# The engines' instruction orders taken from another simulation: one flag of the framework's scheduler in a one-layer bidirectional encoder

## The chip, the core and the metric

The kernel runs on one core of a Trainium2 chip. The core has a matrix engine (PE, with its weight loads shown apart as PEld), a vector engine (DVE), an activation engine (ACT), a general engine (POOL) and a queue engine (SP) that issues transfers. Each engine takes its instructions strictly in the order in which the program gives them, and waits at the head of that order when an input isn't there. The metric is the device time of one execution in microseconds (us), as the median of several runs.

## What is computed

One encoder layer on 256 tokens of width 2048, all in float32, with one residual stream `x`:

```
h = rms_norm(x); proj = h @ w_in            # columns for three mixers and three gates
y_a = spatial_gating(u, v)                  # gMLP, 128-token chunks
y_b = hyena_mixer(b_cols)                   # long two-sided filters, by Fourier transform
y_c = rwkv7_mixer(c_cols)                   # 16 heads, one scan per direction
merged = sum_i sigmoid(gate_i) * (y_i @ w_branch_i)
x = x + merged @ w_out
h = rms_norm(x)
x = x + (silu(h @ w_gate) * (h @ w_up)) @ w_down      # inner width 5632
out = rms_norm(x)
```

## The kernel before

**Weights.** Every dense product reads its weights in pieces of four 128x128 blocks (256 KB). `wsplit` (lines 216 to 229) makes a piece ready: SP loads it into `w` (L221), ACT rounds it to a high half `wh` (L222), and DVE, or POOL for a share of the pieces, subtracts to get the low half `wl` (L226). `w`, `wh` and `wl` have five buffers each. A block then costs PE two or three matmuls: `dense_wide` (L259, L260) does one of 512 columns and one of 256, `dense_sum` the same (L270, L271), `dense` three of 256 (L239 to L241).

**Stages.** The gMLP mixer comes first (L1270 to L1272, then eight `dense_sum` products). Then Hyena: `weave` steps the generators `conv` and `filter_block` in turn, and between their steps lets `fill` trace some dense work of the next projections and merges. Then RWKV: eight groups of two heads go through five generators, `wkv_prep`, `wkv_scores`, `wkv_inverse`, `wkv_chain` and `wkv_norm`; `threads` steps them in turn, and after each step traces about four blocks of dense work (`ROUND = 4.0`). From there on (`merge_last`, `outproj`, `ffn`) it is dense products alone, with their evictions on DVE, ACT and POOL.

**One place in RWKV** that the argument needs. `wkv_inverse` runs a recursion of 15 steps on DVE, two small two-operand instructions a step, and sends its result off with four transfers issued by ACT:

```
z = Yt[:, :w * n].rearrange("p (c t) -> p c t", t=n)
first = V.tensor_tensor(z, ..., mult)                         # L736
V.tensor_tensor(Y[:, :w, k + 1:], Y[:, :w, k + 1:], z, add)    # L739
...
D.dma_start(d2[:, b, :, r, 16 * b:16 * b + 16], Y[...])        # L746, four, on ACT's queue
```

`wkv_norm` of an earlier group subtracts a mean on DVE (L916, after the matmul of L915), squares on ACT (L919), and sums the squares on PE (L921). `threads` steps `wkv_norm` ahead of `wkv_inverse`, so the norm's instructions are traced among those of the recursion.

**Who sets the order.** The kernel is traced instruction by instruction; that gives the program order. When the `TileContext` closes, the framework's list scheduler lays down the final order of each engine: it walks through a simulated time, and an engine that is free in it takes, of its instructions whose inputs and buffers are there in that simulation, the one traced first. So an instruction stands behind a later-traced one where the simulation had the later one ready first. The numbers of the simulation are used for nothing else: the instructions, their engines, their buffers and their semaphores' meaning stay as written. Two pins act on the order: `issue_after` puts what it encloses behind a named instruction of the same engine (in `threads`, every RWKV matmul behind the last dense one traced), and `keep_in_program_order` puts one instruction behind all that its engine has been given so far (L736's first of each recursion, the transposition at L754).

## Time and profile before

| | |
|---|---|
| median of 3 runs | 2004.01 us (2001.47 to 2006.61) |
| the profiled execution's own time | 2002.49 us |
| its span, first to last instruction | 2000.6 us |
| PE busy / PEld busy | 1890.1 us (94%) / 1676.9 us (84%) |
| DVE / ACT / POOL busy | 1389.2 (69%) / 1068.7 (53%) / 545.8 us (27%) |
| moved from HBM | 313.96 MB, 159 GB/s over the span |
| mean granted PE clock | 0.983 |

Busy is the time in which an engine ran at least one instruction. [...] What lies outside the span is 1.9 us of the execution's own time.

### The profile page before, as it was taken

How to read it: one execution, taken by the hardware profiler on the slowest of the kernel's cores; microseconds unless marked ns; L12 is line 12 of the kernel's file. 1: busy time of each engine (PE TensorE's matmuls, PEld its weight loads, DVE VectorE, ACT ScalarE, POOL GpSimd, SP SyncE). 2: the span in 40 equal slices, each digit the busy share in tenths (PEclk: the TensorE clock that was granted, in tenths of full speed). 3: DMA queues.
4: the chain of work that ended last, by engine and by line, in shares of the span. 5: the costliest groups of instructions: out<-in, count | busy, mean ns of one | idle time of the engine just before them, and what ended most of it. 6: DMA issues, size and time to landing. Idle time of an engine off the chain costs nothing.

```text
span 2000.6 us, 37495 instructions
## 1 busy us (share of the span) xinstructions
PE 1890.1 (94%) x13476; PEld 1676.9 (84%) x13476; DVE 1389.2 (69%) x2556; ACT 1068.7 (53%) x2142; POOL 545.8 (27%) x573
## 2 busy tenths in 40 slices
PE   8999999999879888898999999999999999999997
PEld 6788888879878777787898888888888888888886
DVE  7978798786775767667556777766666666655555
ACT  7665566555444454444545555555555555545443
POOL 3322322235654455544421121111111111100001
PEclk9999999999999999999999999999999999999998
DMA  7444444445333333333345565555555555666664
GB/s 259 160 168 150 135 157 154 137 138 187 125 112 94 97 99 97 110 99 91 107 158 186 186 229 189 187 190 190 190 190 190 190 190 190 189 186 186 188 186 136
DMA packets 215827, 320.38 MB, mean 160 GB/s; under 512 B 62198, under 2 KB 65784, under 8 KB 215640
## 3 DMA queue, kind: packets, MB, share of 16 engines
q1 hardware_dynamic: 165744, 301.93, 45.5%
q10 hardware_dynamic: 47864, 9.87, 2.5%
q0 software_dynamic: 2032, 6.18, 1.0%
q8 instruction: 106, 1.74, 0.3%
q14 instruction: 81, 0.66, 0.1%
HBM read 313.96 MB, written 3.93 MB: 159 GB/s over the span
## 4 chain that ended last, share of the span: by engine, by line
PE 50%; DVE 0%; DVEq 0%; ACT 0%; issue 0%; ACTq 0%
PE ps_dn L259 23%; PE ps_dn L260 12%; PE ps_big L259 8%; PE ps_big L260 4%; PE ps_dn L239 0%; PE ps_dn L240 0%; PE ps_dn L241 0%; PE ps_dn L257 0%; PE ps_dn L256 0%; DVE x L1458 0%; PE ps_inv L865 0%; DVEq L1473 0%; PE ps_ch L859 0%; PE ps_big L893 0%; PE ps_big L1415 0%; PE ps_big L898 0%
## 5 line engine op out<-in xcount | busy, mean ns | idle before, releaser
L222 ACT CAST wh<-w 128x512 fp32r<-128x512 f32 x1148 | 704.4, 620 | 569.6 <-PE ps_dn L259 260.0
L226 DVE TENSOR_TENSOR wl<-w,wh 128x512 fp32r<-128x512 f32 x945 | 719.7, 770 | 375.0 <-ACT wh L222 370.7
L226 POOL TENSOR_TENSOR wl<-w,wh 128x512 fp32r<-128x512 f32 x203 | 270.3, 1338 | 370.2 <-ACT wh L222 329.5
L259 PE MATMUL ps_dn<-gw,wh 128*128 128x512 f32 x704 | 246.3, 391 | 0.0
L259 PE MATMUL ps_big<-gw,wh 128*128 128x512 f32 x704 | 246.0, 391 | 0.0
L270 PE MATMUL ps_dn<-hw,wh 128*128 128x512 f32 x640 | 231.9, 401 | 11.9 <-DVE x L400 7.0
L259 PE MATMUL ps_dn<-hid,wh 128*128 128x512 f32 x660 | 233.2, 396 | 0.0
L239 PE MATMUL ps_dn<-hw,wh 128*128 128x256 f32 x688 | 213.4, 310 | 0.0
L241 PE MATMUL ps_dn<-hw,wl 128*128 128x256 f32 x688 | 199.1, 289 | 3.4 <-DVE wl L226 2.6
L240 PE MATMUL ps_dn<-hw,wh 128*128 128x256 f32 x688 | 199.2, 289 | 0.0
L260 PE MATMUL ps_dn<-hid,wl 128*128 128x256 f32 x704 | 198.4, 282 | 0.0
L260 PE MATMUL ps_dn<-gw,wl 128*128 128x256 f32 x704 | 197.3, 280 | 0.0
L260 PE MATMUL ps_big<-gw,wl 128*128 128x256 f32 x704 | 197.1, 280 | 0.0
L271 PE MATMUL ps_dn<-hw,wl 128*128 128x256 f32 x640 | 179.8, 281 | 0.0
L259 PEld LDWEIGHTS ps_dn<-gw,wh 128*128 128x128 f32 x704 | 131.7, 187 | 28.9
L259 PEld LDWEIGHTS ps_big<-gw,wh 128*128 128x128 f32 x704 | 131.6, 187 | 28.9
L270 PEld LDWEIGHTS ps_dn<-hw,wh 128*128 128x128 f32 x640 | 121.1, 189 | 39.6 <-ACT th L1348 5.6
L259 PEld LDWEIGHTS ps_dn<-hid,wh 128*128 128x128 f32 x660 | 124.0, 188 | 30.0
L239 PEld LDWEIGHTS ps_dn<-hw,wh 128*128 128x128 f32 x688 | 134.5, 195 | 6.4 <-issue 2.9
L241 PEld LDWEIGHTS ps_dn<-hw,wl 128*128 128x128 f32 x688 | 134.0, 195 | 4.8 <-DVE wl L226 3.0
L240 PEld LDWEIGHTS ps_dn<-hw,wh 128*128 128x128 f32 x688 | 134.5, 195 | 1.8
L260 PEld LDWEIGHTS ps_dn<-gw,wl 128*128 128x128 f32 x704 | 133.1, 189 | 0.1
(404 smaller groups left out, 3706.9 us busy)
## 6 DMA issues: line engine op xcount, KB each, us to landing
w<-in_wgu_dram SPq DMA_DIRECT2D x352, 256.0 KB, 3.0
w<-in_wgt_dram SPq DMA_DIRECT2D x192, 256.0 KB, 3.0
w<-in_wdn_dram SPq DMA_DIRECT2D x176, 256.0 KB, 2.8
w<-in_wc_dram SPq DMA_DIRECT2D x108, 256.0 KB, 3.0
w<-in_wb_dram SPq DMA_DIRECT2D x96, 256.0 KB, 3.0
w<-in_wbr_dram SPq DMA_DIRECT2D x96, 256.0 KB, 2.7
w<-in_wo_dram SPq DMA_DIRECT2D x64, 256.0 KB, 3.1
w<-in_wav_dram SPq DMA_DIRECT2D x32, 256.0 KB, 3.6
```

The source lines that it names most:

```text
L222: nc.scalar.copy(wh[:, :m], w[:, :m])
L226: e.tensor_tensor(wl[:, :m], w[:, :m], wh[:, :m].bitcast(F32), ALU.subtract)
L239: mm(ps, wh[:, i, :], xh[:, k, :], start=(k == 0), stop=False)
L240: mm(ps, wh[:, i, :], xl[:, k, :], start=False, stop=False)
L241: self.last = mm(ps, wl[:, i, :], xh[:, k, :], start=False, stop=(k == nk - 1))
L259: mm(ps, wh[:, i, :], xk.rearrange("p a t -> p (a t)"), start=(k == 0), stop=False)
L260: mm(ps[:, :T], wl[:, i, :], xk[:, 0, :], start=False, stop=(k == nk - 1))
L270: mm(ps, wh[:, i, :], x[:, k].rearrange("p a t -> p (a t)"), start=(k == 0), stop=False)
L271: mm(ps[:, :T], wl[:, i, :], x[:, k, 0, :], start=False, stop=(k == nk - 1))
```

## The change

One argument of the context is set. The scheduler then walks the timeline simulation, which holds sequencers, engines, transfer queues and PE's clock as separate resources, instead of its plain model. The kernel's text, and so the program order, stays the same.

```
-    with tile.TileContext(nc) as tc:
+    with tile.TileContext(nc, schedule_with_timeline_sim=True) as tc:
         Build(tc, aps, out).run()
```

## Rows read from the trace of the kernel before

**Rows 1.** Stages: window; busy of PE, PEld, DVE, ACT, POOL; granted clock; DMA.

```profile
57.00:128.00 71.00, 64.09 (x355) 54.73 (x355) 61.64 (x137) 45.65 (x93) 25.00 (x27) 0.95 0.46 156
128.00:467.00 339.00, 320.46 (x1938) 282.86 (x1939) 275.49 (x475) 201.50 (x408) 103.01 (x71) 0.99 0.44 149
467.00:1010.00 543.00, 477.35 (x5306) 442.06 (x5305) 363.51 (x800) 254.55 (x575) 284.75 (x303) 0.96 0.36 109
1010.00:1023.00 13.00, 13.00 (x126) 12.58 (x126) 6.90 (x16) 5.37 (x11) 3.60 (x4) 1.00 0.39 131
1023.00:1987.00 964.00, 963.41 (x5555) 845.70 (x5553) 628.43 (x1033) 520.15 (x974) 109.85 (x142) 1.00 0.58 188
```

**Rows 2.** Waits, whole span: who waited for whom; us in total, times, longest.

```profile
ACT wh L222 <- PE ps_dn L259: 260.0, 384, 0.8
```

**Rows 3.** Windows around PE's ten long stalls, columns as in rows 1.

```profile
64.00:77.00 13.00, 8.78 (x35) 7.25 (x34) 13.00 (x39) 7.84 (x19) 7.83 (x11) 0.74 0.24 81
362.00:370.00 8.00, 6.05 (x28) 5.03 (x26) 7.40 (x13) 3.61 (x8) 3.82 (x3) 0.79 0.35 121
442.00:452.00 10.00, 6.66 (x29) 5.49 (x28) 7.56 (x10) 5.05 (x10) 2.54 (x2) 0.83 0.47 164
515.00:527.00 12.00, 6.37 (x41) 5.50 (x39) 10.20 (x15) 2.53 (x5) 8.12 (x10) 0.72 0.27 91
551.00:565.00 14.00, 8.78 (x60) 7.88 (x59) 13.24 (x33) 1.44 (x3) 7.62 (x10) 0.76 0.30 104
597.00:610.00 13.00, 8.92 (x53) 8.54 (x52) 11.07 (x31) 3.06 (x8) 6.66 (x9) 0.74 0.26 76
679.00:691.00 12.00, 6.47 (x32) 5.77 (x32) 8.31 (x25) 2.50 (x5) 3.25 (x4) 0.72 0.34 88
796.00:807.00 11.00, 6.21 (x31) 5.51 (x30) 6.86 (x20) 2.33 (x5) 3.38 (x4) 0.69 0.40 104
843.00:855.00 12.00, 8.88 (x50) 8.50 (x50) 11.86 (x42) 3.07 (x7) 4.81 (x7) 0.72 0.23 79
922.00:934.00 12.00, 8.10 (x63) 7.24 (x66) 8.12 (x23) 2.33 (x5) 4.55 (x5) 0.86 0.45 116
sum 117.00, PE 75.22 PEld 66.72 DVE 97.64 ACT 33.76 POOL 52.59; mean PE 7.52 PEld 6.67 DVE 9.76 ACT 3.38 POOL 5.26
```

**Rows 4.** Waits of PE, whole span, columns as in rows 2.

```profile
PE ps_big L921 <- ACT sq L919: 14.2, 3, 5.5
PE ps_inv L865 <- DVE T L861: 13.0, 8, 4.1
```

**Rows 5.** Timeline 677 to 686, four engines: start, duration, instruction, idle before.

```profile
677.33 0.60 PE L915 MATMUL ps_big<-y,consts 128*128 128x256 f32 x2
...
677.90 1.26 DVE L739 TENSOR_TENSOR Y<-Y,Z 128x32 f32<-128x32 f32 x1
...
680.89 0.19 DVE L739 TENSOR_TENSOR Y<-Y,Z 128x30 f32<-128x30 f32 x1
...
683.06 0.17 DVE L739 TENSOR_TENSOR Y<-Y,Z 128x8 f32<-128x8 f32 x1
683.14 0.41 DVE L916 TENSOR_TENSOR y<-y,ps_big 128x256 f32<-128x256 f32 x1
683.26 1.82 ACTq L746 DMA_DIRECT2D d<-Y  x4
685.12 0.42 ACT L919 ACTIVATE sq<-y 128x256 f32<-128x256 f32 x1 [7.42 <-issue]
...
685.60 0.79 PE L921 MATMUL ps_big<-sq,consts 128*128 128x256 f32 x1 [5.53 <-ACT sq L919]
```

**Rows 6.** Timeline 552 to 558: one step of the recursion beside POOL's work.

```profile
552.61 4.77 DVE L736 TENSOR_TENSOR Z<-Z,Y 128x15 f32<-128x15 f32 x1
...
553.64 3.69 POOL L226 TENSOR_TENSOR wl<-w,wh 128x512 fp32r<-128x512 f32 x3
```

**Rows 7.** L736's instructions: count, duration in ns min/median/max, first and last start.

```profile
L736 DVE TENSOR_TENSOR Z<-Z,Y x120: 161/185/4768, 552.6 to 965.6; 128x30 f32<-128x30 f32 x24, 128x14 f32<-128x14 f32 x16, 128x24 f32<-128x24 f32 x16, 128x15 f32<-128x15 f32 x8
```

## The prediction

> **What bounds the kernel now.** I read the stages first, by windows [rows 1]. The reader is to see two halves. From 1023 to 1987 us PE is busy 963.41 of 964.00 us at full clock: 0.6 us idle. The 13 us before are full too. Everything that PE loses lies in front of that: 6.9 us idle in the gMLP's second part, 18.5 in Hyena and 65.7 in RWKV. Behind 1987 us there is only the final normalization, for which PE has nothing left to do. So PE's work sets the end, and an order can only take away or add stalls of PE, nearly all of them in the first 1010 us.
>
> Then I looked for where those stalls are. Ten places carry most of it [rows 3]: in 117.00 us of windows PE is busy 75.22, so 41.8 us idle. And each long stall is followed by a stretch at half clock: the granted clock of these windows is 0.69 to 0.86, and one minus the clock times the length, summed over the ten, is 28.7 us of full-clock work not done. Together 70.4 us, 7.0 us a place. That is the stake: a stall of 3 to 5 us costs about as much again in clock.
>
> Last, what ends the stalls. The largest entry in PE's waits is L921 for ACT's square, 14.2 us in three waits [rows 4], and these are three of the ten places (679, 796, 922 us). The timeline of the first [rows 5]: the matmul whose result L916 needs ran at 677.33 for 0.60 us, yet L916 runs at 683.14, right after the last L739 of a recursion with which it has nothing to do. Behind it ACT's next instructions are the four issues of L746, which wait for that same recursion and take 1.82 us; only then comes the square at 685.12, and PE stands 5.53 us. Here the order itself is late: L916 is traced among the recursion's steps, so it stands behind the last one only because the plain model had the recursion finished before L915's result came. On the chip DVE was more than 5 us later than in that model, relative to PE.
>
> **The change part by part.** It adds and removes no instruction. What can move, and what each move is worth:
>
> *The dense half, 0 us.* ACT's rounding waits for PE to free buffers 384 times, never over 0.8 us [rows 2], so the weights are ahead of PE by all five buffers. A window of 964 us holds 5555 matmuls, two to a block: 0.35 us a block, 1.4 us a piece, so four spare pieces are 5.6 us of cover. A new order on DVE or ACT would have to hold a split back that long to be seen; if it did in each of the 16 + 44 + 16 columns of `outproj` and `ffn`, every microsecond beyond would cost 76 us. DVE is busy 628 and ACT 520 of 964 us there, so no queue grows, and I take 0. SP's queue holds little but the loads of `w`, each waiting for its buffer in turn, so nothing there is moved past anything; the other issues sit on ACT and POOL between computing work, and those of RWKV (L746) are priced with the stalls.
>
> *The three stalls at L921.* The timeline simulation would have to see that the recursion is slower than the plain model thinks. Undisturbed, a step's instruction takes 0.185 us [rows 7] and the next starts some 0.22 us after it (680.89 to 683.06 us holds ten starts' distance) [rows 5]; 30 of them are 6.6 us, the size of the lateness. If the new simulation prices such short dependent instructions nearer to that, L916 comes ready while the recursion still runs, and goes between two of its steps. Then 14.2 us of waiting go, and the half clock behind them, 0.28 x 12 + 0.31 x 11 + 0.14 x 12 = 8.5 us: 22.7 us. What is late next is L925 and the rest of the norm, which nobody in PE's dense work needs. Bounds: 0 (the order there stays) and 22.7. I take the whole, since five of the eight groups pass this place without a wait already.
>
> *The stalls that a DVE instruction beside POOL makes.* One recursion step takes 4.77 us instead of 0.185 [rows 6], while POOL runs its subtractions, and PE waits behind it; L865's 13.0 us [rows 4] are of this family. An order chosen by durations alone doesn't see it. Bounds: all of the family's four windows (515, 551, 597, 843 us) gone, 28 us; or as many more. I take 0.
>
> [...]
>
> *The gMLP, Hyena and the rest.* DVE is full there (61.64 of 71, 275.49 of 339 us), and the order is by age among ready work; three places, 64, 362 and 442 us. Bounds 21 us either way; I take 0.
>
> *New stalls.* ACT's and DVE's orders in the first half mix the work of several threads, so nearly every instruction there can move, and each place where the new simulation is wrong by 3 us makes a stall of 7.0 us with its clock. Zero to three such is what the count of ten suits; I take one and a half, 10.5 us.
>
> The sum, on the profiled execution: 2002.5 - 22.7 + 10.5 = 1990.3 us. The median of the runs lies 1.5 us above the profiled one, so **1992 us**.
>
> **Rivals.**
> 1. *The trade is even.* The recursion is late because of POOL (one step took 1.26 us there [rows 5]), no simulation of durations sees that, the three stalls stay or come back elsewhere, and nothing else moves by over 6 us. For it: [rows 6]. Against it: the stretch after 680.89 us runs undisturbed and still L916 waits for its end. Time: 1998 to 2010, about 2003.
> 2. *The same jam in all eight groups (slower).* ACT's queue has four issues per group that wait for the recursion. If the new simulation has transfers or recursions done earlier, relative to PE, than the chip, the square of L919 lands behind them in every group, not three. Price 22.7 / 3 = 7.6 us a group: from the fourth group on it is a loss, five more groups are 37.8 us. For it: the mechanism is in the profile. Against it: a model with more of the latencies should err less. Time 2012 to 2042.
> 3. *Dense work used up too early.* If the simulation has the RWKV chain later than the chip, PE is given dense blocks ahead of chain steps, and the stock between 1010 and 1023 us, 13 us [rows 1], is gone when the last group's chain still runs. Beyond 13 us every 10 us taken ahead leave about 10 us of chain with little under it. For it: `issue_after` allows only this direction. Against it: the chain steps of old stand pinned behind their blocks and catch up. 20 to 40 us ahead give 2010 to 2030.
>
> **How the numbers follow.** A measurement of this kernel tells about 0.3%, 6 us, from no change: faster is below 1998, slower above 2010. The forecast's case (the three stalls go, up to two new ones come, 1981 to 1996) has 0.40. More gained (the three go, none comes, two of the other seven places go too: 2004.0 - 22.7 - 14.1 = 1967 us) has 0.07. Even trade 0.19. The jam in more groups 0.20, dense work used up 0.09, several at once and beyond 2042 0.05. So faster 0.47, same 0.19, slower 0.34. The range reaches from the best of the gains, 1967, to the jam in all groups, 2042; the forecast's own is 1981 to 1996.
>
> **What would show it.** Right: no wait of L921 for L919 over 1 us, L916 standing between L736 and L739 in all groups; PE idle between 467 and the RWKV's end near 50 us, not 65.7; the dense half still 964 us long; fewer half-clock windows. Wrong: L921's waits at more groups, idle after ACT's L746; or gaps in PE in the last stretch of RWKV between chain steps with no dense matmul left; or a wait of PE for `wl` in the dense half, which would undo the first step.

## The result, and the profile after

The changed kernel is slower: 2056.84 us (2054.90 to 2060.52, 4 runs) against 2003.22 us in the same session, ratio 1.0252, 95% interval 1.0234 to 1.0271. That is 65 us above the prediction and 15 above the upper end of its range. The profiled execution took 2060.52 us, its span is 2058.6 us at a granted clock of 0.964 (the mean share of its full speed that PE was given; the clock records of both kernels hold 1.0 and 0.5 alone, and half clock is the 0.5).

Windows of the kernel after, by stage, columns as in [rows 1]. The boundaries are the first matmuls of the gMLP's second part, of Hyena and of RWKV; 1013 us is where the last dense work that was to be had ran out, 1092 us where `merge_last` goes on.

```profile
0.00:68.00 68.00, 54.27 (x208) 40.73 (x208) 58.81 (x111) 48.04 (x96) 31.16 (x41) 0.97 0.68 215
68.00:130.00 62.00, 61.81 (x356) 54.35 (x357) 48.96 (x114) 39.26 (x79) 10.07 (x12) 0.97 0.52 175
130.00:481.00 351.00, 326.74 (x1933) 289.28 (x1932) 277.09 (x474) 204.12 (x408) 102.99 (x72) 0.96 0.43 144
481.00:1013.00 532.00, 480.85 (x4779) 445.66 (x4778) 353.02 (x719) 238.51 (x526) 291.60 (x302) 0.95 0.38 115
1013.00:1092.00 79.00, 55.93 (x696) 45.15 (x694) 35.29 (x107) 23.46 (x67) 3.56 (x6) 0.73 0.09 20
1092.00:2046.00 954.00, 953.08 (x5510) 834.48 (x5510) 622.57 (x1025) 517.53 (x967) 108.02 (x140) 1.00 0.59 188
```

The reader is to see three things against [rows 1]. The dense half is as full as before: 953.08 of 954 us, clock 1.00. RWKV begins at 481 us instead of 467. And the 13 full us at its end have become 79 us in which 23 are idle, the clock is 0.73 and DMA moves 20 GB/s: no weights are being loaded, since no dense block is left to load them for.

Summing idle time and clock up to the end of the last dense matmul (1985.9 us before, 2043.9 after), from the traces' matmuls and clock records: idle 96.9 us before, 112.4 after; at half clock 58.0 us in ten stretches before, 139.9 us in 22 after. PE is busy in 46.1 and 123.1 us of that half clock, and half of this, by the clock alone, is lost work: 23.0 and 61.6 us. (A block of L270 and L271 took 0.35 us before the clock fell and 0.64 at half: before, 62 to 75 us.) So of the span's 58.0 us more, 15.5 are idle time, 38.5 are the clock, and about 4 are left as busy time that neither explains.

Waits of the kernel after: four over the whole span, and L921's in the window 1013 to 1092.

```profile
ACT wh L222 <- PE ps_dn L259: 269.3, 394, 1.8
PE ps_inv L865 <- DVE T L861: 15.7, 9, 4.1
PE ps_dn L270 <- DVE x L400: 9.9, 4, 4.1
PE ps_dn L259 <- DVE yc L323: 6.4, 1, 6.4
```

```profile
PE ps_big L921 <- ACT sq L919: 1.0, 1, 1.0
```

L921, the largest entry of [rows 4] with 14.2 us, is down to one wait of 1.0. ACT's rounding still waits for PE, 394 times and never over 1.8 us, the cover of [rows 2]. New is the 6.4 us before the first dense block after RWKV (L259): it waits for the last group's output, as nothing else is there to do.

The stretch without dense work, in windows, and the start of the chain that ended last within it (start, duration, instruction):

```profile
1013.00:1024.50 11.50, 9.82 (x168) 8.54 (x167) 9.00 (x20) 3.01 (x8) 1.33 (x2) 0.71 0.30 90
1024.50:1031.50 7.00, 5.49 (x83) 3.87 (x82) 2.39 (x5) 4.73 (x14) 0.79 (x2) 0.74 0.13 21
1031.50:1055.40 23.90, 19.79 (x174) 17.10 (x174) 8.61 (x41) 4.68 (x14) 0.00 (x0) 0.50 0.12 15
1055.40:1085.50 30.10, 20.75 (x273) 15.59 (x272) 11.04 (x30) 10.03 (x30) 0.72 (x1) 0.89 0.00 1
1085.50:1092.00 6.50, 0.08 (x2) 0.05 (x1) 4.25 (x12) 1.00 (x2) 0.72 (x1) 0.81 0.01 3
```

```profile
1015.46 1.14 PE ps_big L667 x8
...
1033.07 1.99 PE ps_ch L846 x28
1035.73 1.13 PE ps_inv L865 x4
1037.23 1.24 PE ps_inv L878 x4
1038.90 0.80 PE ps_ch L859 x2
...
1072.34 0.72 PE ps_inv L865 x4
1073.54 0.68 PE ps_inv L878 x4
```

At 1015 us the last group's scores (L667) are only beginning. From 1031.5 to 1055.4 us PE is busy for 19.79 of 23.90 us and yet at 0.50 all the way, running dependent chain matmuls alone. The four matmuls of L878 take 1.24 us there and 0.68 at the full clock later. Right behind, from 1055.4 to 1085.5 us, it is chain matmuls alone again, and the clock is mostly full (0.89). Full-clock work done in the 79 us: 55.9 busy, less half of the 35.0 that were busy at half clock, is 38.4. So 40.6 us are lost in this stretch, which is the third rival's mechanism.

### The profile page after: what moved, and what is told of

It reads as the page before. It is cut to its first block, busy times and chain, and to the rows that moved or that the text cites. A ratio compares the mean times of both kernels' runs of the same rounds, so it can differ in the third digit from the quotient of the medians.

```text
span 2058.6 us, 37536 instructions
## 1 busy us (share of the span) xinstructions
PE 1932.7 (94%) x13476; PEld 1709.6 (83%) x13476; DVE 1403.8 (68%) x2556; ACT 1070.9 (52%) x2141; POOL 551.4 (27%) x573
## 4 chain that ended last, share of the span: by engine, by line
PE 80%; DVE 12%; ACT 3%; DMA 2%; issue 2%; POOL 1%; ACTq 0%; DVEq 0%; POOLq 0%
PE ps_dn L259 23%; PE ps_dn L260 12%; PE ps_dn L270 10%; PE ps_big L259 8%; PE ps_dn L271 5%; PE ps_big L260 4%; PE ps_dn L239 3%; PE ps_dn L240 3%; PE ps_dn L241 3%; DVE wl L226 2%; PE ps_big L667 1%; DVE Y L739 1%; DVE Z L736 1%; PE ps_inv L865 1%; DVE ta L627 1%
## 5 line engine op out<-in xcount | busy, mean ns | idle before, releaser
L222 ACT CAST wh<-w 128x512 fp32r<-128x512 f32 x1148 | 707.0, 619 | 626.3 <-PE ps_dn L259 269.3
L226 DVE TENSOR_TENSOR wl<-w,wh 128x512 fp32r<-128x512 f32 x945 | 726.7, 773 | 408.9 <-ACT wh L222 402.3
L226 POOL TENSOR_TENSOR wl<-w,wh 128x512 fp32r<-128x512 f32 x203 | 271.2, 1344 | 360.5 <-ACT wh L222 325.2
L270 PE MATMUL ps_dn<-hw,wh 128*128 128x512 f32 x640 | 237.9, 410 | 13.9 <-DVE x L400 5.8
L259 PE MATMUL ps_dn<-gw,wh 128*128 128x512 f32 x704 | 246.3, 394 | 0.0
L259 PE MATMUL ps_big<-gw,wh 128*128 128x512 f32 x704 | 246.0, 394 | 0.0
L259 PE MATMUL ps_dn<-hid,wh 128*128 128x512 f32 x660 | 230.3, 393 | 0.0
L241 PE MATMUL ps_dn<-hw,wl 128*128 128x256 f32 x688 | 202.9, 295 | 6.7 <-DVE wl L226 6.7
L271 PE MATMUL ps_dn<-hw,wl 128*128 128x256 f32 x640 | 183.3, 286 | 0.0
L270 PEld LDWEIGHTS ps_dn<-hw,wh 128*128 128x128 f32 x640 | 125.1, 195 | 42.8 <-issue 4.4
L259 PEld LDWEIGHTS ps_big<-gw,wh 128*128 128x128 f32 x704 | 132.0, 188 | 30.7
L259 PEld LDWEIGHTS ps_dn<-gw,wh 128*128 128x128 f32 x704 | 132.0, 188 | 30.6
L259 PEld LDWEIGHTS ps_dn<-hid,wh 128*128 128x128 f32 x660 | 124.2, 188 | 28.6
L239 PEld LDWEIGHTS ps_dn<-hw,wh 128*128 128x128 f32 x688 | 136.2, 198 | 10.1 <-issue 4.2
L240 PEld LDWEIGHTS ps_dn<-hw,wh 128*128 128x128 f32 x688 | 136.5, 198 | 2.8 <-issue 1.0
```

The lines of the kernel that those rows point to most:

```text
L222: nc.scalar.copy(wh[:, :m], w[:, :m])
L226: e.tensor_tensor(wl[:, :m], w[:, :m], wh[:, :m].bitcast(F32), ALU.subtract)
L239: mm(ps, wh[:, i, :], xh[:, k, :], start=(k == 0), stop=False)
L240: mm(ps, wh[:, i, :], xl[:, k, :], start=False, stop=False)
L241: self.last = mm(ps, wl[:, i, :], xh[:, k, :], start=False, stop=(k == nk - 1))
L259: mm(ps, wh[:, i, :], xk.rearrange("p a t -> p (a t)"), start=(k == 0), stop=False)
```

## The experiments

**How an order is held.** Several kernels below are traced twice: once to read the order that one model gives, and once to build with it. In the second, each instruction of the named engines gets an edge "behind that one on its engine" (order only, no semaphore); all else is placed by the other model around it. In this code and in that of the reserve below, `NoSync` is short for the order-only kind of dependency.

```
def pin(tc, traced, orders):
    for o in orders.values():
        for a, b in zip(o, o[1:]):
            tc.add_manual_dep(traced[b], traced[a].name, NoSync, reason="order")
```

Theory A: the timeline simulation puts dense blocks ahead on PE, and the open end is the loss (rival 3). Theory B: the new orders of DVE, ACT and POOL hold the RWKV chain back, and PE's order only follows.

**e1_pe_plain.** Timeline simulation, PE in the old order (`keep = ["PE"]`).

> PE takes the old schedule's order, the other engines' orders are laid down by the timeline simulation around it. Theory A (PE is given its dense blocks ahead of the RWKV chain's steps, they are gone when two groups are still to do, and some 80 us of chain lie open): about 2003 us, 1990 to 2015, no stretch without dense matmuls. Theory B (the new orders of DVE, ACT and POOL hold the chain back, PE's order only mirrors that): 2035 us or more, with PE waiting at chain steps for over 100 us in RWKV.

Measured: 2043.55 us, 1.0196 (1.0181 to 1.0211). The dense blocks last to the chain's end, and only some 12 of 53 us come back. Neither theory alone.

**e2_pe_timeline.** The reverse: plain model, PE in the order of the changed kernel.

> The reverse: PE takes the order of the changed kernel, the other engines' orders are laid down by the plain model around it. Theory A: 2040 to 2065 us, with the open stretch of chain at the end of RWKV. Theory B: below 2020 us.

Measured: 2071.87 us, 1.0331 (1.0314 to 1.0348). PE's new order costs more here than together with the orders that were made with it. What mixing two models' orders costs by itself, in either direction, no run measures; e1, e4, e6, e7 and e8 are mixtures too.

**e3_dense_in_place.** The changed kernel with the first matmul of each dense block in RWKV held behind the instruction traced just before it on PE:

```
-                mm(ps, wh[:, i, :], xh[:, k, :], start=(k == 0), stop=False)
+                self.tc.keep_in_program_order(mm(ps, wh[:, i, :], xh[:, k, :], start=(k == 0), stop=False))
```

> Timeline simulation, but in RWKV each dense block's first matmul is pinned behind what is traced before it on PE, so that no dense block passes a chain step. Theory A: the some 44 us lost in RWKV come back and the 14 us lost in gMLP and Hyena stay: 2010 to 2020 us. Theory B: PE waits in place for the late chain, 2040 us or more.

**e5_plain_in_place** is its control: the same line in the kernel before.

> The kernel before (plain model) with each dense block's first matmul of the first half held at its traced place on PE: the control of the kernel with the timeline simulation and the same hold, which took 2058. If the hold by itself costs nothing, this is the kernel before: 2000 to 2008 us, and then the 54 us between the two come from the other instructions' places alone. If the hold is what costs (an order of PE that can't give way to chain steps), this one lands well above, at 2020 to 2060, and the earlier run says nothing about the chain.

Measured: e3 2058.34 us, 1.0271 (1.0256 to 1.0286); e5 2037.57 us, 1.0147 (1.0114 to 1.0179). I first read e3 as the end of theory A. The control says otherwise: the hold costs some 30 us by itself, so e3 decides nothing. (It is an edge to one instruction, the one traced just before on the engine, and not to all before it, as the description ahead of the prediction has it.) With the hold in both, the two models stand 21 us apart by the medians (25 by the ratios) instead of 53. That hints that the dense blocks' places have a part, and no more, since the hold need not cost the same in both.

**e4_pool_plain.** The changed kernel with POOL alone in the old order.

> Only POOL takes the old schedule's order; PE, DVE and ACT are laid down by the timeline simulation. POOL makes a part of the dense pieces' low halves, so a dense block can't pass a chain step by more than POOL's order lets it. Theory A: most of RWKV's loss gone, 2005 to 2030 us. Theory B (DVE's and ACT's new orders at fault): 2035 us or more.

Measured: 2058.22 us, 1.0267 (1.0251 to 1.0282). POOL's order is not the cause.

**e6_dve_act_pool_plain.** DVE, ACT and POOL in the old order (`keep = ["DVE", "Activation", "Pool"]`), only PE placed by the timeline simulation.

> DVE, ACT and POOL take the order of the kernel before; only PE (and the transfers' issues on SP) are placed by the timeline simulation. Theory B (the new orders of DVE, ACT and POOL hold the chain back, and PE's early dense blocks only follow from that): PE's order comes near the old one by itself, and the time is 2000 to 2015 us. Theory A (the timeline simulation puts dense blocks ahead on PE whatever the others do): 2035 to 2060 us, with no dense matmul left after about 1010 us. In between, 2015 to 2035, each has a share.

Measured: 2081.99 us, 1.0365 (1.0325 to 1.0405), the slowest of all, although 792 dense blocks, not 816, stand ahead of the last chain's end (before: 791). Theory B as I had it falls: with the old orders on the other three engines PE's new order costs the most, though this is a mixture as well. Windows of this kernel, its RWKV and two neighbouring stretches in it:

```profile
487.20:1099.20 612.00, 532.78 (x5424) 488.12 (x5424) 363.33 (x806) 253.08 (x584) 288.34 (x306) 0.90 0.34 99
...
924.00:931.00 7.00, 4.84 (x199) 3.93 (x185) 1.15 (x3) 4.15 (x14) 0.00 (x0) 0.99 0.12 32
931.00:938.00 7.00, 6.39 (x25) 5.74 (x26) 4.16 (x9) 3.56 (x8) 4.40 (x5) 0.52 0.45 147
```

About the same matmuls as in [rows 1] (5424 here, 5306 + 126 there) keep PE busy 42 us longer, at a clock of 0.90. From 924 to 931 us PE runs 199 matmuls, nearly all of the chain, and is idle for 2.2 us; behind that the clock is at half. Before, each of the seven half-clock stretches of RWKV followed idle time among dense matmuls; here, in ten of 19, over 40% of the matmuls just before are chain matmuls. The control e15 below has two such of its eleven.

**e7_pe_dve_plain** and **e8_pe_act_plain.** PE and DVE, or PE and ACT, in the old order, the rest by the timeline simulation.

> PE and DVE take the order of the kernel before; ACT and POOL are placed by the timeline simulation. With PE alone held it was 2043.6, 40 us over the kernel before. Theory B1 (those 40 us are DVE's: its instructions stand at the head of their queue before PE's results and transfers have come): 2000 to 2012 us. Theory B2 (they are ACT's and POOL's): 2030 to 2045 us.

> PE and ACT take the order of the kernel before; DVE and POOL are placed by the timeline simulation. Theory B1 (DVE's order costs the 40 us that were left with PE alone held): 2030 to 2050 us. Theory B2 (ACT's order, with its issues of transfers, does): 2000 to 2012 us. If both this and the run with PE and DVE held land at 2015 to 2030, each engine's order has a part.

Measured: 2025.72 us, 1.0085 (1.0054 to 1.0115), and 2027.28 us, 1.0093 (1.0057 to 1.0130). Against e1's 2043.6 each of the two engines' old orders gives back 16 to 18 us by the medians, 21 to 22 by the ratios: both have a part, as the last expectation allowed. In both, RWKV starts 13 and 16 us late.

**e9 to e12: is the old order a lucky one?** Theory C: the order before is a picked one among many, and any other has more stalls and half clock. Theory D: the timeline simulation's orders are worse as such. One constant makes other orders under either model:

```
-ROUND = 4.0
+ROUND = 3.8        # e9 plain, e11 timeline; 4.2 in e10 plain, 3.5 in e12 timeline
```

> The kernel before (plain model) with 3.8 instead of 4.0 dense blocks traced per step of RWKV: another order of RWKV from the same model, that nobody has chosen. Theory D (the timeline simulation's orders are worse than the plain model's as such): 2000 to 2015 us, no more half-clock stretches in RWKV than before, about 7 with 44 us. Theory C (the order before is a picked one of many, and nearly any other one has 12 to 20 half-clock stretches there): 2020 to 2060 us.

> The same with 4.2. Theory D: 2000 to 2015 us. Theory C: 2020 to 2060 us. One of the two near 2005 and the other over 2025 would say that both have a part.

> The changed kernel (timeline simulation) with 3.8 instead of 4.0. Its PE order has still all 816 dense blocks ahead of the chains of the last two groups. If the dense blocks that are gone too early are what costs (rival 3 of the prediction), and the order's luck has no part, it is as slow as the changed kernel, 2045 to 2065 us, like any other of this model. If luck decides (theory C), it may land anywhere from 2010 to 2080, and as often below 2045 as above 2065.

> The changed kernel with 3.5. Fewer dense blocks are traced per step, yet its PE order has all 816 ahead of the last two groups again. Dense work gone too early as the cause: 2045 to 2065 us. Luck of the order: anywhere from 2010 to 2080.

Measured: plain 2012.77 us, 1.0034 (1.0015 to 1.0053), and 2008.12 us, 1.0001 (0.9975 to 1.0026); timeline 2062.55 us, 1.0275 (1.0252 to 1.0299), and 2056.10 us, 1.0243 (1.0223 to 1.0264). Theory C falls: three plain orders lie within 7 us of each other, three timeline orders within 7 us of each other, 43 to 57 us higher. That the half clock would not grow in the plain ones was wrong (68 and 61 us in RWKV, before 44).

**e13 to e16: a reserve of dense blocks, without the price of the hold.** In RWKV every 16th (e14: 48th) dense block is put behind the last matmul that each of the five threads has traced so far:

```
+                self.blocks += 1
+                if self.blocks % 16 == 0:
+                    for b in self.behind.values():      # last PE instruction of each thread
+                        self.tc.add_manual_dep(m.ins, b, NoSync, reason="reserve")
```

e13 and e14 do so under the timeline simulation, e15 under the plain model (the control). e16 instead holds all engines' instructions traced ahead of RWKV in the old order.

> The changed kernel (timeline simulation), in which every 16th dense block of RWKV is held on PE behind the last matmul traced in each of the five RWKV threads; all else is free. PE's order then has 743 and 792 of the 816 dense blocks ahead of the last two chains' ends, as before (735, 791), instead of 816 and 816. Theory R (the dense blocks used up too early cost the 45 us lost in the open tail): the tail is covered again and the time is 2010 to 2030 us, what is left over 2005 being the first two stages. Theory T (the timeline simulation's orders of the chain are bad as such, with or without dense blocks over them): the stalls move ahead of 1010 us, and the time is 2045 to 2075 us.

> The same with every 48th block: 753 and 805 ahead of the last two chains' ends. Theory R: 2010 to 2035 us, within 10 us of the hold at every 16th. Theory T: 2045 to 2075 us.

> Control: the kernel before (plain model) with the hold at every 16th dense block. Its PE order moves by at most 7 blocks at any chain, so if the hold by itself is free the time is 2000 to 2012 us. If it lands above 2020, the hold has a price of its own, as it had with each block's first matmul held (2037.6), which is to be taken off the runs with the timeline simulation.

> All engines' instructions traced ahead of the RWKV threads take the order of the kernel before; RWKV and what follows is placed by the timeline simulation, without a reserve. RWKV then starts near 467 us instead of 481. If the two parts add up (theory R and T alike), 2038 to 2048 us: the 14 us of the first stages come back and the rest stays. If the late start of RWKV is what makes its own order bad, below 2025 us.

Measured: e15 2006.26 us, 1.0000 (0.9987 to 1.0013): this hold is free. e13 2045.15 us, 1.0196 (1.0172 to 1.0220); e14 2060.98 us, 1.0266 (1.0242 to 1.0291); e16 2049.16 us, 1.0214 (1.0191 to 1.0237). Windows of RWKV in the control e15 and in e13:

```profile
466.50:1024.00 557.50, 496.41 (x5425) 460.83 (x5424) 367.72 (x815) 259.25 (x585) 290.44 (x306) 0.94 0.36 109
```

```profile
475.80:1061.40 585.60, 515.60 (x5426) 470.95 (x5424) 369.88 (x811) 257.39 (x583) 292.15 (x306) 0.95 0.35 103
```

With dense blocks to its end, RWKV in e13 is still 28 us longer than in the control: PE is idle 9 us more and busy 19 us more, at nearly the same clock (0.95, 0.94). So the open end, 40.6 us at its own place, was worth 12 us at most: with the reserve most of it is lost earlier, because the chain takes longer anyhow. In e14 the dense blocks last to the chain's end too (1081.1 and 1080.7 us), and nothing is gained; its RWKV has 109 us at half clock. Theory T (bad as such) holds for the larger part, theory R for the smaller, and e14 doesn't confirm even that. e16's RWKV begins at 468 us, 13 us earlier than in the changed kernel, and 8 of them come back (1.0252 to 1.0214, with intervals that touch), less than its expectation had.

**e18_plain_until_rwkv_reserve16.** Both of them together.

> All ahead of RWKV in the order of the kernel before, and in RWKV, placed by the timeline simulation, every 16th dense block held behind the chains. If the two parts add up (7.4 us back from the first, 11.7 from the second, against 2056.8): 2034 to 2042 us, and some 32 us are left to the new order within RWKV, with PE's chain matmuls in fewer and longer runs (about 170 changes from dense to chain instead of 218). If the two were two names for one loss: 2043 to 2050.

```profile
467.80:1065.10 597.30, 526.72 (x5426) 480.58 (x5424) 370.77 (x811) 257.50 (x583) 292.60 (x306) 0.93 0.34 101
```

Measured: 2034.03 us, 1.0146 (1.0118 to 1.0174). The parts add up within the noise: 7.4 us for the first stages and 11.7 for the reserve were expected, 19.1 together; the medians give 22.8 and the ratios 21 (1.0252 to 1.0146), with an interval of some 6 us either way. Some 29 us (0.0146 of 2007) are left to the new order within RWKV.

**e17_plain_norm_moved: the prediction's gain alone.** The order before, held on all engines, but in the three groups where L916 stands behind a recursion it goes behind step six, and L919 ahead of the four issues of L746:

```
+    for late, group, size, room in (("y", "step", 15, 6), ("sq", "move", 4, 0)):
+        ...
+                    o.remove(n)
+                    o.insert(o.index(marks[group][g + room]), n)
```

> The kernel before with its order held instruction for instruction, except that in the three groups where the norm's subtraction (L916) stands behind a recursion it is moved to behind that recursion's step six, and its square (L919) ahead of the four issues of L746 on ACT. That is the prediction's gain alone: the three stalls at L921 with the half clock behind them, 22.7 us. If all of it is real: 1980 to 1988 us. If the wait is only half of it gained, or the clock falls anyway behind another stall: 1988 to 1998. If the stall only moves to what follows the norm: 2000 to 2008.

Measured: 2013.69 us, 1.0035 (1.0018 to 1.0052): slower than every case that I had written down. Its lines stand 4 further down (L763 is L759 of before, L671 L667, L929 L925, L750 L746, L226 L222, L230 L226). Waits of PE, then the timeline of the first of the three places, then windows of it and of the second:

```profile
PE ps_inv L763 <- DVE Z L758: 8.1, 4, 2.6
PE ps_dn L243 <- ACT th L1352: 5.1, 2, 2.8
```

```profile
683.22 1.82 ACTq L750 DMA_DIRECT2D d<-Y  x4
685.13 1.14 ACT L226 CAST wh<-w 128x512 fp32r<-128x512 f32 x2 [5.89 <-issue]
685.78 0.69 DVE L230 TENSOR_TENSOR wl<-w,wh 128x512 fp32r<-128x512 f32 x1 [2.60 <-ACT wh L226]
...
686.39 0.42 DVE L929 TENSOR_SCALAR sq<-ps_big 128x256 f32<-128x256 f32 x1
...
686.87 1.16 PE L671 MATMUL ps_big<-ar,bk 64*128 64x128 f32 x8 [3.37 <-DVE sq L929]
...
691.30 0.43 DVE L758 STREAM_TRANSPOSE Z<-Z 128x256 f32<-128x256 f32 x1
...
691.78 1.08 PE L763 MATMUL ps_inv<-Z,Mo 32*32 32x32 f32 x64 [2.58 <-DVE Z L758]
```

```profile
679.00:691.00 12.00, 6.84 (x50) 6.11 (x48) 8.72 (x26) 2.37 (x5) 3.79 (x4) 0.90 0.47 132
691.00:697.00 6.00, 5.22 (x141) 4.71 (x141) 3.50 (x8) 2.41 (x5) 1.58 (x2) 0.50 0.04 12
796.00:807.00 11.00, 8.20 (x55) 7.53 (x54) 9.47 (x27) 2.45 (x5) 4.01 (x4) 0.90 0.33 80
807.00:822.00 15.00, 12.81 (x180) 11.31 (x179) 8.36 (x14) 6.39 (x17) 4.41 (x6) 0.51 0.22 71
```

No wait of L921 is left, and nothing is gained. At the first place ACT still stands at the issues of L746 until the recursion ends (5.89 us idle), and with it the rounding of weights, DVE's `wl` behind that, and L925 behind `wl`, whose buffer PE's scores need: 3.37 us. Then L759 waits for the recursion's own result: 2.58 us. One stall of 5.53 us [rows 5] has become two. At the other two places PE's first wait is for `th` (L1348 of before, 2.80 and 2.31 us), which ACT also does behind these issues, and its second for the recursion's result again (2.19 and 2.31 us). The half clock behind them is longer: 0.90 and 0.50 in the windows instead of 0.72 and then full. By the records, half clock lasts 10.2, 17.1 and 13.7 us at the three places instead of 6.8, 6.8 and 3.4. All else, L925 too, keeps its old place in this run; an order with the rest of the norm moved as well was not built.

**The runs side by side**, RWKV alone, from the traces: its start, length (to its last matmul), PE's idle time, the time at half clock (us), and how often PE's order goes from dense matmuls to chain matmuls. The first column of times is the median; the others are of the one profiled execution, which lay 9 us above its median in e18, 8 in e10, 6 in e6, 4 in the kernel after, and 6 below it in e13; in e10 and e6 the excess lies in the dense half.

| | median us | start | length | idle | half | changes |
|---|---|---|---|---|---|---|
| before | 2003 to 2007 | 467 | 555 | 66 | 44 | 218 |
| e15 plain, reserve | 2006 | 467 | 558 | 61 | 61 | 224 |
| e10, e9 plain, 4.2, 3.8 | 2008, 2013 | 467, 468 | 559, 566 | 62, 65 | 61, 68 | 215, 215 |
| e7 PE, DVE old | 2026 | 480 | 566 | 69 | 65 | 218 |
| e8 PE, ACT old | 2027 | 483 | 565 | 63 | 68 | 218 |
| e1 PE old | 2044 | 491 | 576 | 71 | 75 | 218 |
| e18 both parts | 2034 | 468 | 597 | 71 | 82 | 178 |
| e13 reserve | 2045 | 476 | 586 | 70 | 58 | 177 |
| after | 2057 | 481 | 604 | 68 | 96 | 170 |
| e6 only PE new | 2082 | 487 | 612 | 79 | 123 | 170 |

Idle time and clock are not all of it. PE's busy time in RWKV, less half of what was busy at half clock, is 470 to 473 us in the seven kernels with an order of the plain model on PE (before, e15, e10, e9, e7, e8, e1), and 483 in e6, 490 in e13 and 489 in e18, for the same 816 blocks and the same chain. So with the timeline simulation's order PE takes 10 to 20 us longer there even at an equal clock. The 28 us between e13 and e15 are 9 us of idle time and 20 of this, with the clock 1 us the other way; the 57 between e6 and the kernel before are 13 of idle time, 33 of clock and 10 of this.

## Why the prediction was wrong

*The dense half, 0 us.* Right: 953.08 of 954 us busy.

*The three stalls at L921, -22.7 us.* The waits went, 14.2 to 1.0 us, and the step was wrong all the same, in its premise and in its worth. I had L916 traced among the recursion's steps, the description ahead of the prediction says so too, and it is not: in every group it is traced behind them, and the new order moved it among them in one group of eight. The waits went because the chain is later: before, L915 ended at 677.9, 794.3 and 921.3 us, while a recursion ran until 683.2, 799.0 and 924.9; after, it ends 1.5 us or more behind one in seven groups, and only in the eighth, the one that was moved, runs within one (854.4 us, recursion from 846.4 to 866.3). And moved by hand, in e17, the gain is none: "What is late next is L925 and the rest of the norm, which nobody in PE's dense work needs" is the sentence that fails. What is late next is what else stands behind ACT's issues (the scores' buffer by way of L925 at one place, `th` at two), and at all three the recursion's own reader, L759.

*The stalls beside POOL, 0 us.* The longest L736 fell from 4.77 [rows 6] to 1.30 us, and L865's waits rose from 13.0 [rows 4] to 15.7. The long steps do stand beside POOL's work: before, the 171 of the 240 instructions of L736 and L739 that overlap no tensor operation of POOL took at most 0.20 us each, the 69 others up to 4.77, with a median of 0.66. What makes them long no run shows.

*The gMLP, Hyena and the rest, 0 (±21).* Within its bounds, but a loss: RWKV starts 14 us later, and e16 gives 8 us back (1.0252 to 1.0214).

*New stalls, +10.5 us.* This is the term that failed. I took one and a half new places at 7.0 us each, from the count of ten long stalls before. The half-clock stretches rose from ten to 22, and idle time and lost clock together from 119.9 to 174.0 us (96.9 + 23.0, 112.4 + 61.6): 54.1 us net, with the 22.7 that I had counted as gained inside it. It was mis-sized because its premise was wrong: "an order can only take away or add stalls of PE". In RWKV PE's gaps of over 1 us are hardly more than before, 22 against 21, and its idle time rose from 66 to 68 us; what grew there is the time at half clock, 44 to 96 us, and 61 of these 96 us begin where over 40% of the matmuls just before are chain matmuls, none of the 44. The price of a place was a little high in turn: the 28.7 us of lost clock also counted half clock in which PE stood idle, and without that it is 23.0, so 6.5 us a place.

*Rival 3, chance 0.09.* Its mechanism is what the trace after shows, beyond the range that I gave it (79 us instead of 13 + 20 to 40), and its price was overrated in turn: with the blocks held back 12 us return in e13 and none in e14. My argument against it, that the chain steps "catch up", was the wrong one; they can't go ahead of their inputs. *Rival 1* and *rival 2* did not come: ACT's square waited in no group as before.

What the runs show of the cause: of the 53 us, 8 come from the stages ahead of RWKV (e16) and up to 12 from dense work used up too early (e13; none by e14; both parts together 21 to 23, e18). Some 29 us are left to the order within RWKV, and are no chance of one order (e9 to e12). They can't be laid to one engine. PE's new order costs 66 and 73 us with the other engines' old or plainly placed orders (e2, e6), but putting PE alone back gives only 12 us (e1), and the other engines' new orders cost 39 us around PE's old one, of which DVE's and ACT's are some 16 to 22 each (e7, e8; late first stages included). How much of each figure is the price of a mixture is open. Why the timeline simulation's order is bad within RWKV is argued and not shown: PE changes between dense and chain matmuls 170 times instead of 218, so that chain matmuls stand in longer runs with nothing between them to cover their latencies. The time in stretches of over 3 us from one dense matmul to the next is 39 us before, 45 in e15 and 60 in e1, against 81 in e13 and 91 in e6. No run changed that alone. e3's hold was too dear to tell.

No version was found that beats the kernel before.

## What to carry to other kernels

A scheduler's order is worth what it does when its simulation is wrong: here the plainer model kept 25 of the 816 dense blocks behind the last chain's end, and the finer one put all of them ahead of the last two chains' ends. Why it did no run shows. When a stall is to be removed, follow the instruction that waits next on every queue that the stall held (here ACT's issues, the weights behind them, the recursion's reader) before booking its time as gained; and give every hold that serves an experiment a control without the change, since one of ours cost 30 us and another nothing.

## What the runs showed of the hardware

The clock weighed more than the stalls. Idle time grew by 15.5 us and lost clock by 38.5; and between e6 and the kernel before there are as many gaps of over 1 us in RWKV (20 and 21), while the time at half clock is 123 against 44 us. Behind two gaps of 3.4 and 2.6 us with 2.3 us between them (e17, 683 to 692) half clock lasted 10.2 us, behind one of 5.5 us [rows 5] 6.8. And PE that runs dependent chain matmuls alone stayed at 0.50 for 23.9 us while it was busy for 19.79 of them; in the 30.1 us behind, again with chain matmuls alone and busy for 20.75, it had 0.89. What tips it from one to the other no run here shows.

Up to the last dense matmul the kernel before was at half clock in ten stretches, 58.0 us, and the kernel after in 22, 139.9 us. The lost clock is 23.0 of 2000.6 us before, 1.2%, and 61.6 of 2058.6 after, 3.0%.

What stood late in an engine's order held up what stood behind it: before, L916 started on DVE at 683.14 us, behind the last L739 (683.06), though its input's matmul, L915, had ended at 677.93 [rows 5]; in e17 ACT stood idle for 5.89 us ahead of the rounding of weights, which its order had behind the issues of L750.
